# Gate and branch matmuls with tokens stationary and 512 weight columns moving

## The chip, the cores and the metric

The kernel runs on one core of one Trainium2 chip. The metric is device time in microseconds (us). TensorE does the matmuls; VectorE (DVE), ScalarE (ACT) and GpSimd (POOL) do the elementwise work; SyncE (SP) issues nearly all transfers. Each engine runs its own instructions in order, and engines wait for one another through semaphores.

## The reference, cut to what matters

Two layers of a hybrid encoder for 256 tokens of 1024 channels. The part of a layer that the change touches:

```python
h = rms_norm(x, g_mix)
... # out_a, out_b, out_c: three attentions of 4 heads; out_d: a convolution module; each (1, 256, 256)
branches = jnp.stack([out_a, out_b, out_c, out_d], axis=2)          # (1, 256, 4, 256)
proj = jnp.einsum('bsnc,ncd->bsnd', branches, w_branch)             # (1, 256, 4, 1024)
gates = jax.nn.sigmoid(h @ w_gate + b_gate).reshape(b, s, 4, 1024)  # w_gate: 1024 x 4096
x = x + jnp.sum(gates * proj, axis=2) @ w_o
hf = rms_norm(x, g_ffn)
x = x + jnp.square(jax.nn.relu(hf @ w_up)) @ w_down                 # 1024 -> 4096 -> 1024
```

All arrays are float32, and a final RMSNorm closes the trunk.

## The kernel before, in words

**Numbers and weights.** Each matrix product is made of three matmuls of float32r parts: a value is split into a high part (hi) and a remainder (lo), and high x high, high x low and low x high are added up in PSUM (`mm3`, lines 120 to 124). `weights` (line 102) brings one weight tile of 128x1024: SP starts the transfer into `raw` (5 buffers), ScalarE copies the high part (`hi`, line 114, 4 buffers), and VectorE subtracts (`lo`, line 115, 4 buffers). While `share[1]` is 2, POOL makes every second `lo`.

**Order of a layer.** The latent projection (`plat`, 4 tiles), the convolution's inputs (w_in tiles 10, 11, 8, 9), query and key tiles (`qk`), the values (4 tiles), the latent attention's up-projections (`mla`), four more `qk` tiles, 32 gate tiles, 8 branch tiles, 8 tiles of the output projection w_o, then the MLP. The order on TensorE is the order in which the code emits it. The other engines' orders are chosen by a list scheduler at build time, which simulates the program, so that an instruction emitted later can stand earlier in its engine's queue.

**Side work by ticks.** From `qk(0)` on, each weight tile ends with `tick()`, which emits the next entry of `side` (lines 675 to 698). The entries hold the twelve attention heads (`scores`, three ticks later `transposes`, one more tick later `weighted`, and the next head every two ticks, from tick A0 = 4 on), small preparations (the turned latents `plt` at ticks 1 to 3, the rotary key's rows `pkr` at 4, the rotary tables `pcs` at 5) and the convolution's taps at ticks 4 to 24, its normalization at 25 to 29. With A0 = 4 there are 31 entries: 13 tiles before the gates and 18 gate tiles carry them. When they are used up, `share[1]` becomes 0 and the branches start.

**Gates.** The normalized input is kept turned, `xg`, with channels in partitions and the 256 tokens as columns. A gate tile is a set of 128 output channels: its weights are stationary, 8 blocks of 128x128, and the 256 tokens move. `gates(g)` makes two such tiles in one PSUM buffer of the pool `pmm` (tag "mm", 4 buffers). VectorE multiplies by the row of token scales `rb` into `Z` (line 717). ScalarE adds the bias, one number per partition, in `sigmoids(m)` (line 722).

**Branches.** `branch(m)` makes 128 output channels of all four branches with one weight tile, again with weights stationary and 256 tokens moving. VectorE multiplies by the gates (line 737), POOL adds the four products (lines 738, 739), ScalarE and VectorE split the sum into `y` (lines 740, 741). With channels in partitions, `y` is already the form that the output projection takes.

**Output projection.** Lines 768 to 788: here blocks of 128 tokens of `y` are stationary and 512 columns of w_o move. Four PSUM buffers of "mm" hold the sums of the two token blocks and two column halves, over four pairs of k.

Other PSUM pools: `psc` ("sc", 1 buffer) and `ppv` ("pv", 1), which attention uses for scores and weighted values, and `pms` ("ms", 2), for turned tiles and small things.

Of the kernel before, what the change touches and what calls it, by code (L numbers as in the profile page):

```python
# [40 lines left out]
LAT = 420  # L41
WCOLS = 1024

C_GMIX, C_GFFN, C_BGATE, C_GQ, C_GKV, C_DW, C_BDW, C_GLN, C_BLN, C_BF = 0, 8, 16, 48, 50, 51, 113, 115, 117, 119
NSMALL = 123


A0 = 4
CONV_FROM, CONV_TO = 4, 25
WARM = 9  # L50

# [16 lines left out]


@with_exitstack  # L70
def hybrid_trunk(ctx: ExitStack, tc: tile.TileContext, xT, xtok, pos, small, gfin, abias, w_lat, w_v, w_in, w_uq, w_ukv,
                 w_gate, w_br, w_o, w_up, w_dn, out):
    nc = tc.nc

# [15 lines left out]
    def nm(s):  # L90
        count[0] += 1
        return f"{s}_{count[0]}"

    def after(inst, other):
        tc.add_manual_dep(inst.ins, other.ins.name,
                          mybir.DependencyInfo(mybir.DependencyClass.NoSync, mybir.DependencyReason.DATA),
                          reason="order")
# [4 lines left out]
    def weights(src, n=WCOLS, pieces=1, between=None):  # L102
        raw = rawp.tile([P, WCOLS], F32, tag="raw", name=nm("raw"))
        hi = whp.tile([P, WCOLS], F32R, tag="hi", name=nm("hi"))
        lo = wlp.tile([P, WCOLS], F32R, tag="lo", name=nm("lo"))
        share[0] += 1
        eng = nc.gpsimd if share[1] and share[0] % share[1] == 0 else nc.vector
        w = n // pieces
        for c in range(0, n, w):
            nc.sync.dma_start(raw[:, c:c + w], src[:, c:c + w])  # L110
            if c == 0 and between is not None:
                between()
        for c in range(0, n, w):
# [211 lines left out]
    for l in range(L):  # L325
        s = sm[l]

        def col(c):
            return s[:, c:c + 1]
# [191 lines left out]
        def conv_silu(prev):  # L521
            xc = cn["xc"]
            sg = tmp.tile([P, 2, T], F32, tag="d1", name=nm("dsg"), bufs=1)
            after(nc.scalar.activation(sg, xc, AF.Sigmoid), prev)
            nc.vector.tensor_tensor(xc, xc, sg, op=ALU.mult)
            nc.scalar.copy(br[0][:, 6:8, :], xc)
            nc.vector.tensor_tensor(br[1][:, 6:8, :], xc, br[0][:, 6:8, :], op=ALU.subtract)
# [177 lines left out]
        qk(4, True)  # L705
        qk(6, False)


        Z = [big.tile([P, 16, T], F32, tag="big", name=nm("Z")) for _ in range(2)]
        y = [None, None]  # L710

        def gates(g):
            ps = new_ps("pgt")
            for i in range(2):
                mtile(ps[:, i * T:(i + 1) * T], w_gate[l, 2 * g + i], xg)
            i = 2 * g % 16
            nc.vector.tensor_tensor(Z[g // 8][:, i:i + 2, :], ps2(ps), bc(rb, 2), op=ALU.mult)

        def sigmoids(m):
            for i in range(4 * m, 4 * m + 4):  # L720
                zt = Z[i // 16][:, i % 16, :]
                after(nc.scalar.activation(zt, zt, AF.Sigmoid, bias=col(C_BGATE + i)), last_exp[0])

        def branch(m):
            if m == 0:
                y[:] = [act.tile([P, 8, T], F32R, tag="qk1", name=nm("yh")),
                        act.tile([P, 8, T], F32R, tag="qk2", name=nm("yl"))]
            w = weights(w_br[l, m])
            yt = tmp.tile([P, 4, T], F32, tag="y4", name=nm("yt"))
            for a in range(2):  # L730
                ps = new_ps("pbr")
                for n in range(2):
                    for k in range(2):
                        i = 2 * (2 * a + n) + k
                        mm3(ps[:, n * T:(n + 1) * T], cols(w, i), part(br, i), k == 0, k == 1)
                i = (4 * m + 2 * a) % 16
                nc.vector.tensor_tensor(yt[:, 2 * a:2 * a + 2, :], ps2(ps), Z[m // 4][:, i:i + 2, :], op=ALU.mult)
            nc.gpsimd.tensor_tensor(yt[:, 0:2, :], yt[:, 0:2, :], yt[:, 2:4, :], op=ALU.add)
            nc.gpsimd.tensor_tensor(yt[:, 0, :], yt[:, 0, :], yt[:, 1, :], op=ALU.add)
            nc.scalar.copy(y[0][:, m, :], yt[:, 0, :])  # L740
            nc.vector.tensor_tensor(y[1][:, m, :], yt[:, 0, :], y[0][:, m, :], op=ALU.subtract)

        nbr = -1
        for g in range(16):
            gates(g)
            if side:
                continue
            share[1] = 0
            if nbr < 0:
                conv_silu(last_exp[0])  # L750
            else:
                branch(nbr)
            nbr += 1
            sigmoids(nbr)
        for m in range(nbr, KT):
            branch(m)
            if m + 1 < KT:
                sigmoids(m + 1)


        def tokens(ps, st, w, j, first, last):

            mm3(ps, st, (w[0][:, j * 512:(j + 1) * 512], w[1][:, j * 512:(j + 1) * 512]), first, last, late_mov=True)
# [1 line left out]
        def block(pair, k, b):  # L765
            return pair[0][:, k, b * P:(b + 1) * P], pair[1][:, k, b * P:(b + 1) * P]

        xg2 = new_xg()
        po = {(b, h): new_ps("po") for h in range(2) for b in range(NB)}

        def joined(b, h):

            xs = X[:, b, h * 512:(h + 1) * 512]
            nc.vector.tensor_tensor(xs, po[b, h], xs, op=ALU.add)

        def gffn(k):
            return col(C_GFFN + k)

        for kp, h in ((0, 0), (0, 1), (1, 0), (1, 1), (2, 0), (2, 1), (3, 0), (3, 1)):
            w = weights(w_o[l, kp, h])  # L780
            for b in range(NB):
                for j in range(2):
                    k = 2 * kp + j
                    tokens(po[b, h], block(y, k, b), w, j, k == 0, k == KT - 1)
                if kp == 3:
                    joined(b, h)
                    if (h, b) == (1, 0):
                        to_features(0, xg2, gffn, pms, "ms")
        v2 = stream_squares()
        rsq = tmp.tile([P, NB], F32, tag="rsq", name=nm("rsq"))  # L790
        nc.vector.reciprocal(rsq, v2)
# [176 lines left out]
```

## Time and profile before

| | us |
|---|---|
| median of 3 runs | 844.85 (843.68 to 844.89) |
| profiled execution | 845.43 |
| its span | 843.6 |
| TensorE busy in the span (matmuls) | 826.0 (98%) |
| VectorE | 569.9 (68%) |
| ScalarE | 450.0 (53%) |
| GpSimd | 152.7 (18%) |

The span is the profiled execution from its first to its last instruction; the rest of its own time lies around it. Matmuls overlap, so the duration of one in the trace is longer than the step from one start to the next; what they cost is read from the steps. PE is TensorE's matmuls and PEld its loads of the stationary operand.

### The profile page before, as it was taken

How to read it: one execution, taken by the hardware profiler on the slowest of the kernel's cores; microseconds unless marked ns; L12 is line 12 of the kernel's file. 1: busy time of each engine (PE TensorE's matmuls, PEld its weight loads, DVE VectorE, ACT ScalarE, POOL GpSimd, SP SyncE). 2: the span in 40 equal slices, each digit the busy share in tenths (PEclk: the TensorE clock that was granted, in tenths of full speed). 3: DMA queues.
4: the chain of work that ended last, by engine and by line, in shares of the span. 5: the costliest groups of instructions: out<-in, count | busy, mean ns of one | idle time of the engine just before them, and what ended most of it. 6: DMA issues, size and time to landing. Idle time of an engine off the chain costs nothing.

```text
span 843.6 us, 14520 instructions
## 1 busy us (share of the span) xinstructions
PE 826.0 (98%) x5646; PEld 759.5 (90%) x5646; DVE 569.9 (68%) x950; ACT 450.0 (53%) x759; POOL 152.7 (18%) x156
## 2 busy tenths in 40 slices
PE   9989999999999999999999999999999999999996
PEld 8969999999889999999899899999998899999994
DVE  7889984787665555555578899557866655555554
ACT  6745646654464444544485764485445554545443
POOL 6524332124200000000004332312331000000000
PEclk9999999999999999999999999999999999999999
DMA  8655433555546555555554544345555555555531
GB/s 281 232 181 181 132 126 126 166 184 185 165 164 198 189 189 186 186 189 187 172 176 161 188 132 145 132 131 174 194 176 200 175 186 190 191 185 186 188 126 50
DMA packets 42549, 145.55 MB, mean 173 GB/s; under 512 B 5104, under 2 KB 7408, under 8 KB 42352
## 3 DMA queue, kind: packets, MB, share of 16 engines
q1 hardware_dynamic: 41904, 142.98, 52.1%
q10 hardware_dynamic: 576, 1.64, 0.5%
q8 instruction: 44, 0.72, 0.4%
q14 instruction: 25, 0.20, 0.1%
HBM read 143.55 MB, written 1.05 MB: 171 GB/s over the span
## 4 chain that ended last, share of the span: by engine, by line
PE 89%; DVE 5%; issue 2%; POOL 1%; ACT 1%; DMA 0%; SPq 0%; POOLq 0%; DVEq 0%; ACTq 0%
PE pgt L122 7%; PE pgt L123 7%; PE pgt L124 7%; PE pu L123 7%; PE pu L124 7%; PE pu L122 7%; PE pd L123 7%; PE pd L122 7%; PE pd L124 7%; PE S L555 2%; DVE lo L115 2%; PE pqk L122 2%; PE pPV L593 2%; PE pqk L123 2%; PE pqk L124 2%
## 5 line engine op out<-in xcount | busy, mean ns | idle before, releaser
L115 DVE TENSOR_TENSOR lo<-raw,hi 128x1024 fp32r<-128x1024 f32 (+3 forms) x241 | 300.5, 1250 | 195.9 <-ACT hi L114 193.9
L114 ACT CAST hi<-raw 128x1024 fp32r<-128x1024 f32 (+2 forms) x273 | 278.5, 1024 | 266.0 <-issue 208.0
L122 PE MATMUL pgt<-xgh,hi 128*128 128x256 f32 x512 | 149.5, 292 | 0.0
L122 PE MATMUL pu<-xgh,hi 128*128 128x256 f32 x512 | 144.9, 283 | 0.7 <-ACT xgh L293 0.7
L123 PE MATMUL pu<-xgl,hi 128*128 128x256 f32 x512 | 145.1, 283 | 0.3
L124 PE MATMUL pu<-xgh,lo 128*128 128x256 f32 x512 | 144.9, 283 | 0.0
L123 PE MATMUL pgt<-xgl,hi 128*128 128x256 f32 x512 | 144.7, 283 | 0.0
L124 PE MATMUL pgt<-xgh,lo 128*128 128x256 f32 x512 | 144.7, 283 | 0.0
L122 PE MATMUL pd<-hi,u 128*128 128x512 f32 x256 | 100.8, 394 | 1.6 <-ACT u L803 1.6
L123 PE MATMUL pd<-hi,u 128*128 128x512 f32 x256 | 100.7, 393 | 1.1 <-DVE u L804 1.1
L122 PEld LDWEIGHTS pu<-xgh,hi 128*128 128x128 f32 x512 | 98.0, 191 | 3.4 <-ACT xgh L293 1.1
L123 PEld LDWEIGHTS pu<-xgl,hi 128*128 128x128 f32 x512 | 98.0, 191 | 3.0 <-DVE xgl L294 0.7
L124 PE MATMUL pd<-lo,u 128*128 128x512 f32 x256 | 99.6, 389 | 0.0
L122 PEld LDWEIGHTS pgt<-xgh,hi 128*128 128x128 f32 x512 | 97.9, 191 | 0.8 <-issue 0.3
L123 PEld LDWEIGHTS pgt<-xgl,hi 128*128 128x128 f32 x512 | 98.1, 192 | 0.4
L124 PEld LDWEIGHTS pu<-xgh,lo 128*128 128x128 f32 x512 | 98.0, 191 | 0.0
L124 PEld LDWEIGHTS pgt<-xgh,lo 128*128 128x128 f32 x512 | 97.9, 191 | 0.0
L115 POOL TENSOR_TENSOR lo<-raw,hi 128x1024 fp32r<-128x1024 f32 (+1 forms) x32 | 77.4, 2419 | 111.2 <-ACT hi L114 106.5
L491 DVE SCALAR_TENSOR_TENSOR cacc<-up,sm,cacc 128x256 f32<-128x256 f32 x120 | 77.9, 693 | 0.0
L122 PEld LDWEIGHTS pd<-hi,u 128*128 128x128 f32 x256 | 48.3, 189 | 10.8 <-ACT u L803 2.4
L124 PEld LDWEIGHTS pd<-lo,u 128*128 128x128 f32 x256 | 48.1, 188 | 10.4
L123 PEld LDWEIGHTS pd<-hi,u 128*128 128x128 f32 x256 | 48.3, 189 | 9.7 <-DVE u L804 2.0
(255 smaller groups left out, 1358.3 us busy)
## 6 DMA issues: line engine op xcount, KB each, us to landing
raw<-in_w_gate SPq DMA_DIRECT2D x64, 512.0 KB, 3.7
raw<-in_w_up SPq DMA_DIRECT2D x64, 512.0 KB, 4.2
raw<-in_w_dn SPq DMA_DIRECT2D x64, 512.0 KB, 4.2
raw<-in_w_in SPq DMA_DIRECT2D x23, 512.0 KB, 4.2
raw<-in_w_br SPq DMA_DIRECT2D x16, 512.0 KB, 3.7
raw<-in_w_o SPq DMA_DIRECT2D x16, 512.0 KB, 4.3
raw<-in_w_v SPq DMA_DIRECT2D x8, 512.0 KB, 4.2
raw<-in_w_lat SPq DMA_DIRECT2D x8, 210.0 KB, 4.6
```

The source lines that it names most:

```text
L114: cut = nc.scalar.copy(hi[:, c:c + w], raw[:, c:c + w])
L115: done = eng.tensor_tensor(lo[:, c:c + w], raw[:, c:c + w], hi[:, c:c + w], op=ALU.subtract)
L122: nc.tensor.matmul(ps, sh, mh, start=first, stop=False)
L123: nc.tensor.matmul(ps, *((sl, mh) if late_mov else (sh, ml)), start=False, stop=False)
L124: nc.tensor.matmul(ps, *((sh, ml) if late_mov else (sl, mh)), start=False, stop=last)
L491: ins = nc.vector.scalar_tensor_tensor(cacc[:, c, :], up[:, c, j:j + T], wcol, cacc[:, c, :], op0=ALU.mult, op1=ALU.add)
L555: nc.tensor.matmul(sl, q[:, b * P:(b + 1) * P], k[:, 0:n], start=True, stop=True)
L593: nc.tensor.matmul(po[o:o + 64, 0:T], v[:, 0, vo:vo + HD], pts[:, 0:T], start=True, stop=False)
```

## The change

The gates and the branches take the form of the output projection: token blocks of 128 are stationary, 512 weight columns move, and the results have tokens in partitions. `gates(c, i)` makes column half c of branch i's gate with four weight tiles into two PSUM buffers; VectorE scales each by the tokens' column `rc` and adds the bias, which now lies along the columns: a tile `bg` of 128x512, one buffer, brought by SP right after the set's first weight tile is asked for. `sigmoid` is one instruction for a set. `branch(c, i)` uses one weight tile, PSUM buffers of "sc" and "pv" (even i) or "ms" (odd i). The sum over the branches is made by POOL for i = 1 and 2 and by VectorE for i = 3. Since the output projection wants channels in partitions, `turned(c)` turns the sums by transposes on TensorE, 8 for each half, and ScalarE and VectorE split them into `y`. The turn of half 0 follows the last set of gates, that of half 1 follows four tiles of the output projection. A0 is 6 instead of 4: attention begins two weight tiles later, the entries of `side` become 33, and 20 gate tiles carry the last of them.

```diff
-A0 = 4
+A0 = 6
...
+        def tokens(ps, st, w, j, first, last):
+            mm3(ps, st, (w[0][:, j * 512:(j + 1) * 512], w[1][:, j * 512:(j + 1) * 512]), first, last, late_mov=True)
+        def block(pair, k, b):
+            return pair[0][:, k, b * P:(b + 1) * P], pair[1][:, k, b * P:(b + 1) * P]
...
-        def gates(g):
-            ps = new_ps("pgt")
-            for i in range(2):
-                mtile(ps[:, i * T:(i + 1) * T], w_gate[l, 2 * g + i], xg)
-            i = 2 * g % 16
-            nc.vector.tensor_tensor(Z[g // 8][:, i:i + 2, :], ps2(ps), bc(rb, 2), op=ALU.mult)
...
+        Z = [big.tile([P, 4, NB, 512], F32, tag="big", name=nm("Z")) for _ in range(2)]
+        def gates(c, i):
+            ps = [new_ps("pgt") for _ in range(NB)]
+            bg = tmp.tile([P, 512], F32, tag="bg", name=nm("bg"), bufs=1)
+            for kp in range(4):
+                w = weights(w_gate[l, c, i, kp])
+                if kp == 0:
+                    nc.sync.dma_start(bg, bgate[l, c, i])
+                for b in range(NB):
+                    for j in range(2):
+                        k = 2 * kp + j
+                        tokens(ps[b], block(xg, k, b), w, j, k == 0, k == KT - 1)
+                tick()
+            for b in range(NB):
+                nc.vector.scalar_tensor_tensor(Z[c][:, i, b, :], ps[b], rc[:, b:b + 1], bg, op0=ALU.mult, op1=ALU.add)
+        def sigmoid(c, i):
+            after(nc.scalar.activation(Z[c][:, i], Z[c][:, i], AF.Sigmoid), last_exp[0])
+        def branch(c, i):
+            pools = (((psc, "sc"), (ppv, "pv")), ((pms, "ms"), (pms, "ms")))[i % 2]
+            ps = [pool.tile([P, 512], F32, tag=tag, name=nm("pbr")) for pool, tag in pools]
+            w = weights(w_br[l, c, i])
+            for b in range(NB):
+                for j in range(2):
+                    tokens(ps[b], block(br, 2 * i + j, b), w, j, j == 0, j == 1)
+                nc.vector.tensor_tensor(Z[c][:, i, b, :], ps[b], Z[c][:, i, b, :], op=ALU.mult)
+                if i == 3:
+                    nc.vector.tensor_tensor(Z[c][:, 0, b, :], Z[c][:, 0, b, :], Z[c][:, 3, b, :], op=ALU.add)
+            if i in (1, 2):
+                nc.gpsimd.tensor_tensor(Z[c][:, 0], Z[c][:, 0], Z[c][:, i], op=ALU.add)
+        def turned(c):
...
+            for pr in range(2):
+                pt = pms.tile([P, 512], F32, tag="ms", name=nm("pyt"))
+                for j in range(2):
+                    o = (2 * pr + j) * P
+                    for b in range(NB):
+                        nc.tensor.transpose(pt[:, j * T + b * P:j * T + (b + 1) * P], Z[c][:, 0, b, o:o + P], ident)
+                ks = slice(4 * c + 2 * pr, 4 * c + 2 * pr + 2)
+                nc.scalar.copy(y[0][:, ks, :], ps2(pt))
+                nc.vector.tensor_tensor(y[1][:, ks, :], ps2(pt), y[0][:, ks, :], op=ALU.subtract)
...
+        raw_gates, todo = [], [(0, i) for i in range(4)]
+        for c, i in [(c, i) for c in range(2) for i in range(4)]:
+            gates(c, i)
+            raw_gates.append((c, i))
+            if side:
+                continue
+            first = share[1] != 0
+            if first:
+                share[1] = 0
                 conv_silu(last_exp[0])
+            while raw_gates:
+                sigmoid(*raw_gates.pop(0))
+            if first:
+                continue
+            for _ in range(2):
+                if todo:
+                    branch(*todo.pop(0))
+        turned(0)
...
+        branch(1, 0)
+        branch(1, 1)
+        output(0, 0)
+        branch(1, 2)
+        branch(1, 3)
+        output(0, 1)
+        output(1, 0)
+        output(1, 1)
+        turned(1)
+        for kp, h in ((2, 0), (2, 1), (3, 0), (3, 1)):
+            output(kp, h)
```

`output(kp, h)` is the body of the former loop over w_o's tiles; its PSUM buffers are now taken one by one, at kp = 0. On the host w_gate, w_branch and the bias are laid out for the new tiles, and the bias leaves the table of small constants.

## Rows read from the trace of the kernel before

**Rows 1.** The profile page, chain that ended last: shares by engine.
```profile
PE 89%; DVE 5%; issue 2%; POOL 1%; ACT 1%; DMA 0%; SPq 0%; POOLq 0%; DVEq 0%; ACTq 0%
```

**Rows 2.** Busy time by stretch: start:end, length, busy us by engine, clock, DMA.
```profile
46.00:50.00 4.00, 0.71 (x4) 0.28 (x2) 4.00 (x6) 1.04 (x1) 1.31 (x1) 1.00 0.26 85
154.00:191.00 37.00, 37.00 (x309) 36.75 (x308) 28.58 (x32) 20.11 (x29) 9.53 (x7) 1.00 0.54 174
```

**Rows 3.** Groups of instructions by shape: count | busy us, mean ns | idle before.
```profile
L122 PE MATMUL pgt<-xgh,hi 128*128 128x256 f32 x512 | 149.5, 292 | 0.0
...
L122 PE MATMUL pbr<-brh,hi 128*128 128x256 f32 x128 | 36.2, 283 | 0.0
```

**Rows 4.** Timeline of TensorE in gates: start us, us, instruction.
```profile
189.78 0.28 PE L122 MATMUL pgt<-xgh,hi 128*128 128x256 f32 x1
...
194.70 0.28 PE L124 MATMUL pgt<-xgh,lo 128*128 128x256 f32 x1
```

**Rows 5.** Timeline of TensorE in the output projection and at transposes of X.
```profile
221.63 0.40 PE L124 MATMUL po<-lo,yh 128*128 128x512 f32 x1
...
223.25 0.39 PE L122 MATMUL po<-hi,yh 128*128 128x512 f32 x1
...
238.66 0.39 PE L124 MATMUL po<-lo,yh 128*128 128x512 f32 x1
238.90 1.03 PE L303 MATMUL pt<-ident,X 128*128 128x128 f32 x8
239.69 0.48 PE L122 MATMUL po<-hi,yh 128*128 128x512 f32 x1
240.00 0.39 PE L123 MATMUL po<-hi,yl 128*128 128x512 f32 x1
```

**Rows 6.** Timeline of ScalarE after those transposes.
```profile
239.53 0.91 ACT L293 ACTIVATE xgh<-pt,sm 128x256 fp32r<-128x256 f32 x2 [0.97 <-PE pt L303]
```

**Rows 7.** ScalarE's copies of 512 columns, line 526: ns min/median/max.
```profile
L526 ACT CAST brh<-xc x2: 607/607/607, 156.2 to 566.8; 128x512 fp32r<-128x512 f32 x2
```

**Rows 8.** Instructions of tile yt: ns min/median/max, first and last start.
```profile
L737 DVE TENSOR_TENSOR yt<-pbr,Z x32: 677/682/691, 162.6 to 631.5; 128x512 f32<-128x512 f32 x32
L738 POOL TENSOR_TENSOR yt<-yt x16: 1292/1296/2378, 164.1 to 632.3; 128x512 f32<-128x512 f32 x16
```

**Rows 9.** Timeline of VectorE after the transposes of X.
```profile
240.34 0.87 DVE L294 SCALAR_TENSOR_TENSOR xgl<-pt,sm,xgh 128x256 fp32r<-128x256 f32 x2
```

**Rows 10.** Timeline of TensorE where the output projection starts.
```profile
220.38 0.39 PE L124 MATMUL po<-lo,yh 128*128 128x512 f32 x1
221.09 0.47 PE L122 MATMUL po<-hi,yh 128*128 128x512 f32 x1 [0.31 <-DVE yt L737]
```

**Rows 11.** Timeline of SP's queue in layer 0 (stretch, instructions merged).
```profile
43.84 5.72 SPq L110 DMA_DIRECT2D raw<-in_w_in  x3
53.13 0.33 SPq L558 DMA_DIRECT2D bt<-in_abias  x1
```

**Rows 12.** Timeline of SP's queue, the output weights of layer 0.
```profile
197.55 20.27 SPq L110 DMA_DIRECT2D raw<-in_w_o  x8
```

**Rows 13.** Timeline of TensorE at the first scores of layer 0.
```profile
46.23 0.39 PE L124 MATMUL pv<-lo,xgh 128*128 128x512 f32 x1
49.91 0.92 PE L555 MATMUL S<-qkA 64*128 64x128 f32 x4 [3.29 <-DVE qkA L636]
...
51.26 0.63 PE L123 MATMUL pv<-hi,xgl 128*128 128x512 f32 x1
...
54.67 0.40 PE L122 MATMUL pv<-hi,xgh 128*128 128x512 f32 x1
```

**Rows 14.** Timeline of VectorE before these scores.
```profile
38.20 3.35 DVE L115 TENSOR_TENSOR lo<-raw,hi 128x1024 fp32r<-128x1024 f32 x1
...
48.65 0.47 DVE L294 SCALAR_TENSOR_TENSOR latl<-plt,sm,lath 128x256 fp32r<-128x256 f32 x1
```

**Rows 15.** The profile page, transfers: count, KB each, us to landing.
```profile
raw<-in_w_gate SPq DMA_DIRECT2D x64, 512.0 KB, 3.7
```

More of the change, by code (lines that the diff above doesn't have):

```diff
@@ L42 @@
 WCOLS = 1024
-C_GMIX, C_GFFN, C_BGATE, C_GQ, C_GKV, C_DW, C_BDW, C_GLN, C_BLN, C_BF = 0, 8, 16, 48, 50, 51, 113, 115, 117, 119
-NSMALL = 123
-A0 = 4
+C_GMIX, C_GFFN, C_GQ, C_GKV, C_DW, C_BDW, C_GLN, C_BLN, C_BF = 0, 8, 16, 18, 19, 81, 83, 85, 87
+NSMALL = 91
+A0 = 6
 CONV_FROM, CONV_TO = 4, 25
@@ L70, in hybrid_trunk @@
 @with_exitstack
-def hybrid_trunk(ctx: ExitStack, tc: tile.TileContext, xT, xtok, pos, small, gfin, abias, w_lat, w_v, w_in, w_uq, w_ukv,
+def hybrid_trunk(ctx: ExitStack, tc: tile.TileContext, xT, xtok, pos, small, gfin, bgate, abias, w_lat, w_v, w_in, w_uq, w_ukv,
                  w_gate, w_br, w_o, w_up, w_dn, out):
@@ L706, in hybrid_trunk @@
         qk(6, False)
-        Z = [big.tile([P, 16, T], F32, tag="big", name=nm("Z")) for _ in range(2)]
-        y = [None, None]
-        def gates(g):
-            ps = new_ps("pgt")
-            for i in range(2):
-                mtile(ps[:, i * T:(i + 1) * T], w_gate[l, 2 * g + i], xg)
-            i = 2 * g % 16
-            nc.vector.tensor_tensor(Z[g // 8][:, i:i + 2, :], ps2(ps), bc(rb, 2), op=ALU.mult)
[L719 to L758, printed above, removed]
         def tokens(ps, st, w, j, first, last):
@@ L766, in block @@
             return pair[0][:, k, b * P:(b + 1) * P], pair[1][:, k, b * P:(b + 1) * P]
+        Z = [big.tile([P, 4, NB, 512], F32, tag="big", name=nm("Z")) for _ in range(2)]
+        y = []
+        def gates(c, i):
[12 more added lines that the diff above has]
+                nc.vector.scalar_tensor_tensor(Z[c][:, i, b, :], ps[b], rc[:, b:b + 1], bg, op0=ALU.mult, op1=ALU.add)
@@ new lines, in turned @@
+        def turned(c):
+            if c == 0:
+                y[:] = [act.tile([P, 8, T], F32R, tag="qk1", name=nm("yh")),
+                        act.tile([P, 8, T], F32R, tag="qk2", name=nm("yl"))]
+            for pr in range(2):
[7 more added lines that the diff above has]
+                nc.vector.tensor_tensor(y[1][:, ks, :], ps2(pt), y[0][:, ks, :], op=ALU.subtract)
@@ new lines, in hybrid_trunk @@
+        raw_gates, todo = [], [(0, i) for i in range(4)]
[7 more added lines that the diff above has]
+                share[1] = 0
+                conv_silu(last_exp[0])
+            while raw_gates:
[5 more added lines that the diff above has]
+                    branch(*todo.pop(0))
@@ L768, in hybrid_trunk @@
+        assert not todo
+        turned(0)
         xg2 = new_xg()
-        po = {(b, h): new_ps("po") for h in range(2) for b in range(NB)}
+        po = {}
         def joined(b, h):
@@ L774, in joined, with output @@
             nc.vector.tensor_tensor(xs, po[b, h], xs, op=ALU.add)
-        def gffn(k):
-            return col(C_GFFN + k)
-        for kp, h in ((0, 0), (0, 1), (1, 0), (1, 1), (2, 0), (2, 1), (3, 0), (3, 1)):
+        def output(kp, h):
             w = weights(w_o[l, kp, h])
             for b in range(NB):
+                if kp == 0:
+                    po[b, h] = new_ps("po")
                 for j in range(2):
@@ L788, in hybrid_trunk, with gffn @@
                         to_features(0, xg2, gffn, pms, "ms")
+        def gffn(k):
+            return col(C_GFFN + k)
+        branch(1, 0)
[9 more added lines that the diff above has]
+            output(kp, h)
         v2 = stream_squares()
@@ L940 @@
     ukv = np.concatenate([ukv[..., :HD].reshape(L, P, 256), ukv[..., HD:].reshape(L, P, 256)], axis=2)
-    gate = A(w_gate).reshape(L, KT, P, 4, KT, P).transpose(0, 4, 3, 2, 1, 5).reshape(L, 32, P, D)
-    bgate = A(b_gate).reshape(L, 4, KT, P).transpose(0, 3, 2, 1).reshape(L, P, 32)
-    brw = A(w_branch).reshape(L, 4, 2, P, KT, P).transpose(0, 4, 3, 1, 2, 5).reshape(L, KT, P, D)
+    gate = A(w_gate).reshape(L, 4, 2, P, 4, 2, 512).transpose(0, 5, 4, 1, 3, 2, 6).reshape(L, 2, 4, 4, P, D)
+    bgate = A(b_gate).reshape(L, 4, 2, 512).transpose(0, 2, 1, 3)[:, :, :, None, :]
+    bgate = np.broadcast_to(bgate, (L, 2, 4, P, 512))
+    brw = A(w_branch).reshape(L, 4, 2, P, 2, 512).transpose(0, 4, 1, 3, 2, 5).reshape(L, 2, 4, P, D)
     dn = A(w_down).reshape(L, FT, P, D)
@@ L948 @@
     bf = np.broadcast_to(A(b_forget)[:, None, :], (L, P, HEADS))
-    small = np.concatenate([pk(g_mix), pk(g_ffn), bgate, pk(g_q_lat), pk(g_kv_lat), dw, pk(b_dw), pk(g_conv_ln),
+    small = np.concatenate([pk(g_mix), pk(g_ffn), pk(g_q_lat), pk(g_kv_lat), dw, pk(b_dw), pk(g_conv_ln),
                             pk(b_conv_ln), bf], axis=2)
@@ L956 @@
         xT=A(x).reshape(T, KT, P).transpose(2, 1, 0), xtok=A(x).reshape(NB, P, D).transpose(1, 0, 2), pos=A(positions).reshape(NB, P).T, small=small,
-        gfin=np.broadcast_to(A(g_final)[None], (P, D)), abias=abias, w_lat=wlat, w_v=wv, w_in=win_t, w_uq=uq, w_ukv=ukv, w_gate=gate,
+        gfin=np.broadcast_to(A(g_final)[None], (P, D)), bgate=bgate, abias=abias, w_lat=wlat, w_v=wv, w_in=win_t, w_uq=uq, w_ukv=ukv, w_gate=gate,
         w_br=brw, w_o=wo, w_up=wt(w_up), w_dn=dn)
```

## The prediction

> **What bounds the kernel now.** I read the chain of waits first: 89% of what ended last is TensorE, so the time is TensorE's instructions plus the few places where it waits [rows 1]. Then the stretches: from 154 to 191 us, gates and branches alone, TensorE is busy all 37 us and VectorE 28.58 of them, so VectorE has a quarter to spare; from 46 to 50 us TensorE works only 0.71 us while VectorE works all 4 [rows 2]. So in the changed stages the pace of single matmuls counts, and in one place of layer 0 VectorE's backlog.
>
> **Gates and branches, 512 columns instead of 256.** Before: 512 gate matmuls in each of three groups, 1536, and 3 x 128 = 384 branch matmuls, all of 256 columns [rows 3]. After: a set has 4 x 2 x 2 x 3 = 48 matmuls of 512, with 8 sets and 2 layers 768; a branch 2 x 2 x 3 = 12, in all 192. The columns streamed stay the same, 960 instructions go.
> The price of one is from its start to the next start, since matmuls overlap. Gates: 189.78 to 194.70 in 41 steps, 0.120 us [rows 4]. The output projection already has tokens stationary and 512 columns moving, the form that the gates take: 223.25 to 238.66 in 68 steps, 0.2266; just before, 221.63 to 223.25 in 7 steps, 0.2314 [rows 5]. At 2.4 GHz 256 and 512 columns are 106.7 and 213.3 ns, so both forms carry some 13 ns beyond their columns, and one of two such remainders goes. Per pair 0.240 - 0.2266 = 13.4 ns, or 8.6 ns at the slower stretch; I take 12 ns, since only a few steps are at the slower pace. 960 x 12 ns = 11.5 us gained (8.3 to 12.9).
> The Trainium skill speaks against this size: "TensorE: Matmul & The Clock Gate", section "Back-to-back issue gap", gives 262 cycles for 256 columns and 518 for 512, so 6 cycles or 2.5 ns a pair; as an estimate from that page the gain would be 2.4 us and the sum about 846 us. The trace does not agree: 120 ns and 227 ns stand where the page's cycles make 109 and 216.
>
> **The sums turned by TensorE.** New: per layer 2 x 8 transposes of 128x128. The same 8 transposes of X between output matmuls run from 238.90 to 239.69, and the step after them is 0.31 instead of 0.227: 0.88 us for 8 [rows 5]. Four such groups: 3.5 us added, and nothing of it beside other work of TensorE.
> After turned(0) TensorE goes on with branch(1,0), which does not need y; output(0,0), which does, comes two weight tiles (5.4 us) later. Branch(1,1) wants the two "ms" buffers of turned(0) 2.7 us (12 matmuls) later; two copies and two subtractions fit in. I cost that at nothing; without the cover it is about the wait of turned(1).
> After turned(1) output(2,0) needs its result at once. In the like place the transposes start at 238.90 and ScalarE's copy at 239.53 [rows 5, 6], 0.63 later; a 512-wide copy takes 0.607 [rows 7], a 512-wide operation of VectorE 0.68 [rows 8]. High part ready 1.24 us after the start, low part some 2.0; TensorE is free after 0.85 and asks for the low part one matmul after the high one: 0.4 + 0.6 = 1.0 us of wait with both engines free. In the like place VectorE began 1.44 us after the transposes [rows 9]; a weight copy and a weight subtraction in front (twice a 512-wide one, 1.2 us each) would add 2.2. I take 1.7, nearer to the free case, twice: 3.4 us added (2.0 to 6.4).
>
> **Waits for the sums.** Turned(1) needs branch(1,3)'s products, POOL's two 1024-wide adds and VectorE's last two adds. From the end of branch(1,1) to turned(1) TensorE has six weight tiles, 6 x 12 x 0.2266 = 16.3 us. POOL's 512-wide add takes 1.3, at worst 2.38 us [rows 8]; two of double width 5.2 to 9.5. With 2.2 us ahead of them (a product behind a weight subtraction) and 3.8 behind (two adds of 0.68, each behind one), 11 to 15.5 us. It fits: nothing. Turned(0) has a whole set, 11 us, more.
> VectorE's other work: as many evictions and products as before, a layer's 8 splits of 256 become 4 of 512, and 4 adds are new (2.7 us); the spare quarter hides them [rows 2]. ScalarE's 32 sigmoids of 256 a layer become 8 of 1024, less work. Without that cover 2.7 us a layer would show. The smaller table of constants changes only a transfer at the start.
>
> **The wait that goes at the end.** Before, the output projection takes all four "mm" buffers while branch(7) still holds one: 220.38 to 221.09 is 0.71 instead of 0.23, 0.48 us [rows 10]. Branches now use other buffers. Two layers: 0.95 us gained (0 to 0.95).
>
> **The bias rows on SP's queue.** 16 new transfers of 256 KB go into a single buffer. Each waits until the set before has been evicted, and the weights behind it on SP wait too, and for them the two halves and TensorE. SP's order is not the program's: the third bias of attention stands in the program ahead of the four w_in tiles of qk(4) and qk(6), yet three w_in were issued from 43.84 on and it at 53.13 [rows 11]. And SP is far ahead: the first output weight was issued at 197.55 [rows 12], while its twelfth matmul starts at 220.38 [rows 10]. So a wait of a few us on SP is covered, and the bias itself has a set (11 us) to land. I take nothing; without cover, see the last rival.
>
> **Attention two tiles later.** In layer 0 TensorE waits from 46.46 to 49.91 for the first scores, 3.45 us, behind VectorE's qkA; then 8 matmuls take 0.427 us each, 512 columns at 1.2 GHz, 1.6 us more: 5.05 in all [rows 13]. With scores two tiles later this wait goes. What is late next: pkr's transposes, which now come first after that tile. They need a "ms" buffer, which plt's second tile holds until its latl ends, 48.65 + 0.47 = 49.12 [rows 14]. If VectorE's order there (a lo that took 3.35 us, then taps of the convolution) stays, TensorE still waits 2.65 us and only 0.8 us is gained, with the lower clock perhaps avoided. I take 2.0, nearer to that end (0.7 to 5.05). The tiles that carry attention grow from 31 to 33: work is moved, none added, and conv_silu and the branches begin after set 5, with their own time on TensorE unchanged.
>
> **The sum**, against the profiled run's own 845.43 us (span 843.6): -11.5 + 3.5 + 3.4 - 0.95 - 2.0 = -7.55, so 837.9; the median of the three runs is 844.85, 0.58 lower, so 837.3. I say 837. All ends for it: 844.85 - 12.9 + 3.5 + 2.0 - 0.95 - 5.05 = 831.5; all against: 844.85 - 8.3 + 3.5 + 6.4 - 0.7 = 845.8.
>
> **Rivals.**
> A, the wide matmuls don't pay: in the gates, beside more work of the other engines, they run at 0.2314 or slower, as the seven steps of the output do [rows 5]. At 0.2314 throughout 8.3 us remain and the time is 840.5, the edge of my own range; at 0.240, as long as two narrow ones, nothing remains: 848.8. Half way: 844.5. For it: the slower stretch exists. Against it: 68 steps at 0.2266.
> B, layer 0's wait goes wholly, with the clock: 3.05 us more, 834; with quick turns (2.0 instead of 3.4) 832.5. For it: a clear late comer, qkA, is taken off the path. Against it: the "ms" buffer at 49.12.
> C, slower: turned(1) waits for the sums. Every us by which the 11 to 15.5 us exceed the 16.3 us of cover is a us of TensorE, in each layer; it turns the sign from 4 us on. With 5 us and the lower clock behind it (1.6 us, rows 13) twice: 13 us, 850. For it: with adds of POOL at 2.38 us less than 1 us of cover is left. Against it: most take 1.3.
> D, slower: the bias transfer stands on SP ahead of its set's second to fourth tiles, so these are issued only after the set before is evicted: 1 us for that, 3.7 for the transfer [rows 15], 1.2 and 1.2 for the halves, less 2.7 for the tile in hand: 4.4 us a set, 16 sets, 70 us: 907. For it: it is so in the program. Against it: the order in rows 11.
>
> **How the numbers follow.** The likeliest 0.52 (own range 834.5 to 840.5), A 0.12, B 0.22, C 0.09, D 0.05. Some 0.2% (1.7 us) is what a measurement of this kernel can tell from no change. Faster: 0.52 + 0.22 + half of A = 0.80; the rest of A is 0.05 within and 0.01 slower; C and D are 0.14 slower. The range 831 to 846 leaves out C and D and the far end of A.
>
> **What would show it.** Gate steps of 0.227, 768 of them, and branch steps alike. Eight transposes in 0.8 us twice a layer; no wait after the first group, 1 to 3 us before the output matmul after the second. Layer 0's wait at 46.5 shorter, ended by latl and not by qkA, and 1.2 GHz after it or not. No wait of TensorE on a weight's halves in the gates. The prediction is wrong if steps of 512 columns in the gates lie above 0.232, if TensorE waits over 3 us at a turn, or if a bias transfer on SP stands before a gap of TensorE.

## The result, and the profile after

The changed kernel takes 849.63 us (median; 848.85 to 850.43) against 844.87 beside it: ratio 1.0059 [1.0041, 1.0076]. It is slower, where I forecast 837 (831 to 846). Its profiled execution has 849.28 us, span 847.5, of which TensorE is busy for 820.7 (97%): 5 us less work, and 9 us more in which it has none.

TensorE's waits in the changed kernel (us in total, times, longest):

```profile
PE pqk L124 <- POOL lo L115: 4.8, 1, 4.8
PE pPV L593 <- ACT pts L584: 3.2, 3, 1.2
PE po L123 <- DVE yl L763: 1.7, 2, 0.9
...
PE po L122 <- ACT yh L762: 1.0, 2, 0.5
```

The wait for qkA [rows 13] and the one where the output projection starts [rows 10] are gone. The two on `po` are turned(1), expected. The two longest were in no step of mine: a weight's low part from GpSimd, and the weighted values of attention.

The matmuls themselves did what was expected. Groups by shape (count | busy us, mean ns | idle before), where [rows 3] had 512 and 128 per line with 256 columns:

```profile
L122 PE MATMUL pgt<-hi,xgh 128*128 128x512 f32 x256 | 106.1, 415 | 0.0
...
L122 PE MATMUL pbr<-hi,brh 128*128 128x512 f32 x64 | 25.1, 392 | 0.0
...
L748 POOL TENSOR_TENSOR Z<-Z 128x1024 f32<-128x1024 f32 x8 | 20.8, 2600 | 123.6 <-DVE Z L744 101.1 <-ACT hi L114 22.5
```

TensorE's timeline in the gates, first beside attention, then after it, and at the two turns (start us, us, instruction, [idle before <- releaser]):

```profile
109.20 0.39 PE L123 MATMUL pgt<-hi,xgl 128*128 128x512 f32 x1
...
111.50 0.39 PE L124 MATMUL pgt<-lo,xgh 128*128 128x512 f32 x1
...
178.90 0.39 PE L122 MATMUL pgt<-hi,xgh 128*128 128x512 f32 x1
...
189.55 0.39 PE L124 MATMUL pgt<-lo,xgh 128*128 128x512 f32 x1
...
206.10 1.03 PE L760 MATMUL pyt<-ident,Z 128*128 128x128 f32 x8
206.89 0.48 PE L122 MATMUL pbr<-hi,brh 128*128 128x512 f32 x1
...
228.76 1.03 PE L760 MATMUL pyt<-ident,Z 128*128 128x128 f32 x8
230.31 0.51 PE L122 MATMUL po<-hi,yh 128*128 128x512 f32 x1 [0.52 <-ACT yh L762]
231.68 0.50 PE L123 MATMUL po<-hi,yl 128*128 128x512 f32 x1 [0.87 <-DVE yl L763]
```

47 steps from 178.90 to 189.55 make 0.2266 us each, and beside attention 10 steps from 109.20 to 111.50 make 0.230 (the 512-column pace of [rows 5], against 0.120 for 256 [rows 4]). After the first turn nothing waits: 0.79 us for 8 transposes, as in [rows 5]. After the second, 0.68 us lie between the transposes' 0.87 and the high part's matmul, and the step behind it is 1.37 instead of 0.227: 1.82 us a layer.

The loss starts in layer 0, in the second tile of qk(2). TensorE's timeline, and two windows of the same place (columns as in [rows 2], TensorE's, its weight loads', then the other engines' busy time, clock, DMA):

```profile
41.22 0.28 PE L123 MATMUL pqk<-xgl,hi 128*128 128x256 f32 x1
46.34 0.58 PE L124 MATMUL pqk<-xgh,lo 128*128 128x256 f32 x1 [4.85 <-POOL lo L115]
...
48.64 0.41 PE L122 MATMUL pqk<-xgh,hi 128*128 128x256 f32 x1
48.86 0.41 PE L123 MATMUL pqk<-xgl,hi 128*128 128x256 f32 x1
```

```profile
46.00:50.00 4.00, 3.66 (x19) 3.66 (x20) 0.00 (x0) 0.00 (x0) 2.62 (x2) 0.57 0.67 201
41.00:46.00 5.00, 0.49 (x5) 0.29 (x3) 3.09 (x6) 1.42 (x2) 2.38 (x3) 1.00 0.33 126
```

A step of 5.12 us stands where 0.12 is usual, and for some 3 us afterwards the granted clock is at the 1.2 GHz level: 0.21 us a step. Together about 6.5 us; the 5.05 us of [rows 13] are gone. The reason is in GpSimd's queue, and behind it in SyncE's. First the changed kernel, GpSimd and SyncE:

```profile
38.57 0.23 POOL L560 MEMSET bt<- 64x64 f32 x2 [5.51 <-DMA bt<-in_abias]
43.62 0.23 POOL L560 MEMSET bt<- 64x64 f32 x2 [4.82 <-DMA bt<-in_abias]
43.81 4.80 POOL L115 TENSOR_TENSOR lo<-raw,hi 128x1024 fp32r<-128x1024 f32 x2
```

```profile
29.26 3.87 SPq L110 DMA_DIRECT2D raw<-in_w_v  x3
33.18 0.44 SPq L558 DMA_DIRECT2D bt<-in_abias  x1
35.96 0.33 SPq L110 DMA_DIRECT2D raw<-in_w_v  x1
36.34 0.43 SPq L558 DMA_DIRECT2D bt<-in_abias  x1
```

Then the same two queues of the kernel before:

```profile
33.10 0.23 POOL L560 MEMSET bt<- 64x64 f32 x2 [0.50 <-DMA bt<-in_abias]
37.86 0.23 POOL L560 MEMSET bt<- 64x64 f32 x2 [4.53 <-DMA bt<-in_abias]
38.06 5.75 POOL L115 TENSOR_TENSOR lo<-raw,hi 128x1024 fp32r<-128x1024 f32 x2
```

```profile
29.18 0.42 SPq L558 DMA_DIRECT2D bt<-in_abias  x1
30.06 2.61 SPq L110 DMA_DIRECT2D raw<-in_w_v  x2
32.72 0.43 SPq L558 DMA_DIRECT2D bt<-in_abias  x1
```

In both kernels the planner put the masking of the first two heads' bias (`bt`) ahead of the low part that qk(2) wants. Before, both biases were issued by 32.72 and the low parts began at 38.06, in time. With attention two tiles later the first bias stands behind two more weight tiles on SyncE and the second behind one more; they are issued at 33.18 and 36.34, the second takes 7.2 us to land instead of 5.1, and the low parts begin at 43.81.

The other loss is at the weighted values, in both layers. TensorE, VectorE and ScalarE of the changed kernel in layer 1:

```profile
493.39 0.28 PE L124 MATMUL pqk<-xgh,lo 128*128 128x256 f32 x1
494.88 0.65 PE L593 MATMUL pPV<-pts,VAC 128*64 128x256 f32 x2 [1.22 <-ACT pts L584]
...
498.34 0.63 PE L123 MATMUL pgt<-hi,xgl 128*128 128x512 f32 x1
498.77 0.63 PE L124 MATMUL pgt<-lo,xgh 128*128 128x512 f32 x1
```

```profile
487.11 3.41 DVE L491 SCALAR_TENSOR_TENSOR cacc<-up,sm,cacc 128x256 f32<-128x256 f32 x3
490.44 1.72 DVE L634 SCALAR_TENSOR_TENSOR QC<-pqk,rb 64x256 f32<-64x256 f32 x4
492.20 0.29 DVE L570 CUSTOM_DVE_ANT_0 neg<-S,bt 128x128 f32<-128x128 f32 x1
```

```profile
492.53 0.40 ACT L572 ACTIVATE pe<-neg,mn 128x128 f32<-128x128 f32 x1 [5.74 <-DVE mn L570]
...
494.36 0.47 ACT L584 COPY pts<-pT 128x384 f32<-128x384 f32 x1
```

VectorE does three taps of the convolution and four evictions of QC before the next head's scores. ScalarE stands 5.74 us before that head's exp, and the copy `pts` of the head before, which TensorE wants at 493.5, is queued behind it. Price: 1.38 us here and at 82.6 us, 1.0 at 114.6, and in layer 1 a stretch at the 1.2 GHz level (0.43 us a step), 1.7 us more. In the kernel before, VectorE reached the scores emitted with the same weight tile after 2.1 us of such work instead of 5.1:

```profile
485.51 1.26 DVE L491 SCALAR_TENSOR_TENSOR cacc<-up,sm,cacc 128x256 f32<-128x256 f32 x3
486.69 0.85 DVE L634 SCALAR_TENSOR_TENSOR QC<-pqk,rb 64x256 f32<-64x256 f32 x2
487.58 0.29 DVE L570 CUSTOM_DVE_ANT_0 neg<-S,bt 128x128 f32<-128x128 f32 x1
```

Of the 3.0 us more, 0.9 are two more evictions of QC. The other 2.1 are the first of the three taps alone: in the changed kernel it starts just behind the start of a low part on GpSimd, which runs until 489.45, and ends only after it, at 489.73; the two taps behind it take 0.48 us each. In the kernel before, the low part starts when the taps are over, at 486.76, and the evictions beside it keep their 0.43 us. First GpSimd and VectorE of the changed kernel, then GpSimd of the kernel before:

```profile
487.06 2.39 POOL L115 TENSOR_TENSOR lo<-raw,hi 128x1024 fp32r<-128x1024 f32 x1
487.11 2.62 DVE L491 SCALAR_TENSOR_TENSOR cacc<-up,sm,cacc 128x256 f32<-128x256 f32 x1
```

```profile
486.76 2.40 POOL L115 TENSOR_TENSOR lo<-raw,hi 128x1024 fp32r<-128x1024 f32 x1 [3.90 <-ACT hi L114]
```

### The profile page after: what moved, and what is told of

The parts are those of the page before. It is cut to its first block, busy times and chain, and to the rows that moved or that the text cites. A ratio compares the mean times of both kernels' runs of the same rounds, so it can differ in the third digit from the quotient of the medians.

```text
span 847.5 us, 12604 instructions
## 1 busy us (share of the span) xinstructions
PE 820.7 (97%) x4718; PEld 710.5 (84%) x4718; DVE 579.4 (68%) x948; ACT 438.2 (52%) x703; POOL 132.2 (16%) x134
## 5 line engine op out<-in xcount | busy, mean ns | idle before, releaser
L122 PE MATMUL pgt<-hi,xgh 128*128 128x512 f32 x256 | 106.1, 415 | 0.0
L123 PE MATMUL pgt<-hi,xgl 128*128 128x512 f32 x256 | 100.5, 393 | 0.0
L124 PE MATMUL pgt<-lo,xgh 128*128 128x512 f32 x256 | 100.5, 393 | 0.0
L115 POOL TENSOR_TENSOR lo<-raw,hi 128x1024 fp32r<-128x1024 f32 (+1 forms) x34 | 81.0, 2384 | 109.5 <-ACT hi L114 104.8
L491 DVE SCALAR_TENSOR_TENSOR cacc<-up,sm,cacc 128x256 f32<-128x256 f32 x120 | 83.2, 735 | 0.0
L124 PEld LDWEIGHTS pgt<-lo,xgh 128*128 128x128 f32 x256 | 48.5, 189 | 11.0
L122 PEld LDWEIGHTS pgt<-hi,xgh 128*128 128x128 f32 x256 | 48.5, 189 | 10.5 <-issue 1.3
L123 PEld LDWEIGHTS pgt<-hi,xgl 128*128 128x128 f32 x256 | 48.6, 190 | 9.2
```

What stands on the lines that cost most here:

```text
L491: ins = nc.vector.scalar_tensor_tensor(cacc[:, c, :], up[:, c, j:j + T], wcol, cacc[:, c, :], op0=ALU.mult, op1=ALU.add)
```

## The experiments

Each ratio is to the kernel before on the same chip, with its 95% interval; "us" is the median.

**Attention back at 4.** The change with one number undone.

```diff
-A0 = 6
+A0 = 4
```

> The changed kernel with A0 = 4 again. Theory 1 (attention two tiles later made the loss): the waits of the changed kernel at 41 us (5.0 us on POOL's lo and 1.6 us of lower clock), at the weighted values (1.3, 1.0, 1.3 us) and the lower clock of layer 1 (1.7 us) go, and the 5.05 us wait for the first scores comes back: 849.6 less 6.5, 842 to 844. Theory 2 (the bias rows' 4 MB and their waits on SP delay the other transfers, or the wide gates don't pay; A0 matters little): 848 to 850, with waits of TensorE on weights.

Measured: 840.31 us, ratio 0.9944 [0.9926, 0.9963]. The waits for GpSimd's low part and at the weighted values are gone; qkA's is back at 1.85 us, with the lower clock behind it, and is TensorE's longest wait:

```profile
PE S L555 <- DVE qkA L636: 1.9, 1, 1.9
```

So the new tiling gains, and A0 alone costs 1.0059 - 0.9944 = 1.15%, 9.7 us.

**A0 = 6 in the kernel before.** The other half of the same split.

```diff
-A0 = 4
+A0 = 6
```

> The kernel before with A0 = 6 alone, nothing else of the change. Theory 1: the same new waits without the new gates: in layer 0 a wait of about 5 us on POOL's lo in place of the one for the first scores, waits of about 1 us at the weighted values, a lower clock in one or two places: 846 to 851. Theory 2: no new wait, 844 to 845, or 840 if the old wait goes and nothing follows.

Measured: 857.75 us, 1.0146 [1.0127, 1.0165]: 12.3 us, more than any theory had. The wait on GpSimd's low part is there at 5.6 us, with eight waits at the weighted values, 6.4 us together, and the clock stays at the 1.2 GHz level for longer (from 46 to 52 us at least, a granted clock of 0.50). A0's cost does not need the new tiles.

**The bias early.** The first two heads' bias loaded and masked before w_in's tile 11.

```diff
+        for h in range(2):
+            bts[h] = load_bias(h)
...
-                bt = tmp.tile([P, 3 * P], F32, tag="bt", name=nm("bt"))
-                nc.sync.dma_start(bt, abias[l, h])
...
+                bt = bts.pop(h) if h in bts else load_bias(h)
```

> The changed kernel (A0 = 6) with the attention biases of heads 0 and 1 loaded and masked before w_in tile 11, so that POOL does not stand behind their transfers. Theory 1: the wait at 41 us and its lower clock go (6.6 us), two transfers of 192 KB more at the start cost up to 1.4: 843 to 845; the waits at the weighted values stay. Theory 2: POOL's lo comes late because the weights land late: the wait stays, 848 to 851.

Measured: 846.43 us, 1.0011 [0.9997, 1.0025]. The wait on the low part went, and in its place TensorE waits for the "ms" buffers, by its timeline:

```profile
45.29 0.44 PE L426 MATMUL plt<-ident,qn 128*128 128x128 f32 x2 [1.17 <-DVE latl L294]
50.80 0.44 PE L449 MATMUL pkr<-ident,kr 128*128 128x128 f32 x2 [2.32 <-DVE latl L294]
```

The second is the wait that the prediction named (latl before pkr): it was right about what is late next in VectorE's chain and blind to GpSimd's, which came first.

**The second turn one tile earlier.**

```diff
-        output(1, 1)
         turned(1)
+        output(1, 1)
```

> The changed kernel with the second turn before the last of the four output tiles instead of after it. The sums were complete at 224.0 us, the turn would start at 226.0 instead of 228.7. Theory 1 on the turn (copy and subtraction are the wait): both waits of 1.86 us go, 845.5 to 846.5. Rival (the sums are late, VectorE behind POOL): the wait moves to the front of the transposes, 849 to 850.

Measured: 845.46 us, 1.0005 [0.9993, 1.0016]: 0.54% or 4.6 us less than the change, both waits on `po` gone. They are 3.7 us in the trace, within the intervals.

**The taps two ticks later as well.**

```diff
-CONV_FROM, CONV_TO = 4, 25
+CONV_FROM, CONV_TO = 6, 27
```

> The changed kernel (849.3 us beside a kernel before of 845.4) with attention still at tick 6, and the convolution's taps moved two ticks later as well (ticks 6 to 26 instead of 4 to 24), so that taps and heads keep the distance that they had before the change. Theory 1 (of the about 9 us that A0 = 6 costs, the lo on GpSimd that stands behind the bias of the heads is 5.0 us with 1.6 us of lower clock, and the waits at the weighted values, 1.4 and 1.0 us in each layer, come from VectorE's order, in which taps and all four evictions of QC stand ahead of a head's scores): the wait of 5 us at 41.2 us stays, and the waits at 82.6, 114.6 and 493.4 us shrink only in so far as the taps make them, because the evictions of QC still stand ahead: 846 to 849 us. Rival (it is the distance between taps and heads that was lost): all waits at the weighted values go with the lower clock after them in layer 1: about 843 us.

Measured: 851.38 us, 1.0074 [1.0057, 1.0090]. No better than the change, perhaps a little worse. The waits at the weighted values are six instead of three, 5.7 us in all. VectorE's order ahead of the head's scores is the same three taps, the first of them behind a low part of GpSimd, and four evictions. Moving the ticks of the taps did not change the order that the planner made; whether that order is what costs is tried further down.

**Attention at 4 with the earlier turn, and then with the taps from 6 on.** Two kernels; the second has both edits and this one.

```diff
-CONV_FROM, CONV_TO = 4, 25
+CONV_FROM, CONV_TO = 6, 25
```

> The changed kernel with attention at tick 4 as before the change (840.3 us) and the second half of the sums turned one tile of the output projection earlier, so that the last such tile stands between the transposes and the matmul that needs their result. Theory 1 (the two measures touch different places and add up; the turn's wait and its slow first step are 1.86 us a layer): 836.6 us. Rival (the sums are now wanted 2.7 us sooner and TensorE waits for GpSimd's adds instead): 840 us or more.

> The kernel with attention at tick 4 and the second turn one tile earlier (theory: 836.6 us), and the convolution's taps from tick 6 on instead of 4 (62 taps over 19 ticks), so that fewer taps stand ahead of qkA's eviction on VectorE in layer 0. Theory 1 (the 2.0 us at the first scores with the 1.6 us of lower clock behind it are VectorE's backlog of taps): both go, 833 us. Rival (the wait moves to the next tile that wants an "ms" buffer, as in the run with the bias early): 835 to 838 us.

Measured: 838.23 us, 0.9918 [0.9902, 0.9934], and 834.77 us, 0.9880 [0.9861, 0.9898]. The two measures add up, though 2.2 us are left of the 3.7; in the trace of the first kernel a wait of 0.68 us for one of GpSimd's low parts is new. In the second kernel the wait for qkA is shorter, not gone (1.38 us instead of 1.87).

**Without the bias rows**, at A0 = 4; the gates' bias is left out.

```diff
+    bg = cst.tile([P, 512], F32, name="bg")
+    nc.gpsimd.memset(bg, 0.0)
...
-            bg = tmp.tile([P, 512], F32, tag="bg", name=nm("bg"), bufs=1)
...
-                    nc.sync.dma_start(bg, bgate[l, c, i])
```

> The changed kernel with attention at tick 4 (840.3 us), without the 16 transfers of the gates' bias rows: the bias is left out of the gates (a constant tile of zeros is added in its place). It prices the transfers on SyncE's queue, which I put at nothing. Theory 1: 840.3 us within 1 us. Rival (the transfers delay weights somewhere): 837 to 838.5 us.

Measured: 842.50 us, 0.9975 [0.9963, 0.9986], slower than with the bias. The trace has a new wait of 2.0 us at the start, on GpSimd's sums, which the tile of zeros now stands ahead of; without it the run would be where the other was, 840.5. The experiment brought its own cost, so it does not price the transfers by itself. With the trace of the changed kernel, in which no matmul of the gates waits for a weight, I take them as hidden.

**Low parts ahead of the bias masks on GpSimd**, A0 = 6. One order edge; SyncE's order stays the changed kernel's.

```diff
-                    nc.gpsimd.memset(bt[...], NEG)
+                    after(nc.gpsimd.memset(bt[...], NEG), pool_lo[0])
```

> The changed kernel (A0 = 6, 849.3 us beside a kernel before of 844.9) with one order edge on GpSimd alone: the memsets that mask a head's bias stand behind every lo that the program emitted before them, as the program has it. SyncE's order stays that of the changed kernel. Theory 1 (the 5.0 us at 41.2 us come from GpSimd's queue, in which those memsets wait for the bias while the lo of a weight stands behind them): this wait goes (with its 1.6 us of lower clock), and the next late comer, the "ms" buffers that plt and pkr need, shows as in the run with the bias early, 1.3 and 2.5 us: 846 to 848 us. If nothing is late behind it: 843 us. Rival (the lo is late for another reason, its raw tile lands too late): no change, 849 us. The waits at the weighted values stay in each case.

Measured: 843.55 us, 0.9980 [0.9971, 0.9989]: 6.7 us less than the change (1.0059 - 0.9980 = 0.79%). GpSimd's queue, where the low parts now begin 6.4 us sooner and the mask follows them (the numbers of lines are 1 to 3 higher in this kernel):

```profile
37.44 5.83 POOL L116 TENSOR_TENSOR lo<-raw,hi 128x1024 fp32r<-128x1024 f32 x2 [4.35 <-ACT hi L115]
43.20 0.23 POOL L563 MEMSET bt<- 64x64 f32 x2
```

TensorE's wait in qk(2) is gone, with SyncE issuing the two biases when it did before (33.21 and 36.38). This shows the first cause: GpSimd's order, not late weights. The edge names nothing else, but the planner shifted VectorE's order a little with it: the waits at the weighted values are four instead of three, 3.1 us against 3.2. The "ms" waits hardly came (0.21 us); another did, 1.67 us for qkB at 62.8 us.

**Scores ahead of QC and KC on VectorE**, A0 = 6.

```diff
+                    if last_neg[0] is not None:
+                        after(ins, last_neg[0])
```

(after each eviction of qk; `last_neg` is the last head's scores emitted.)

> The changed kernel (849.3 us) with order edges on VectorE: the evictions of QC and KC stand behind the scores of the last head emitted before them. Taps are left as they are. Theory 1 (the four evictions of QC ahead of head 2's scores, 1.72 us, are what makes TensorE wait 1.38 us at 82.6 and 493.4 us): both waits go, with the lower clock after the second (1.7 us); the wait at 114.6 us and the 5.0 us at 41.2 us stay: 844.5 to 846.5 us. Rival (the taps, slowed to 1.1 us each by GpSimd's lo, are enough by themselves): the waits stay at about 1 us, 848 to 849 us.

Measured: 849.04 us, 1.0055 [1.0038, 1.0071]. The rival was right. VectorE's order shows why:

```profile
486.95 4.59 DVE L492 SCALAR_TENSOR_TENSOR cacc<-up,sm,cacc 128x256 f32<-128x256 f32 x6
491.46 0.28 DVE L572 CUSTOM_DVE_ANT_0 neg<-S,bt 128x128 f32<-128x128 f32 x1
```

Three more taps took the place of the evictions; the scores come 0.74 us sooner, and the two waits only halve (1.22 to 0.62 and 0.66 us of idle time), while one of 0.82 us is new at 526 us. The rival's reason was not quite right: the six taps take 4.59 us because the first stands behind GpSimd's low part (2.61), and the others take 0.47 each.

**Scores ahead of the taps too**, the same edge in `conv`.

> As the run before (QC and KC behind the scores), with the convolution's taps also behind the scores of the last head emitted before them. Theory 1 (what stands ahead of a head's scores on VectorE is the whole of the waits at the weighted values): all of these go, 1.0 us a layer more than in the run before, and the 5.0 us at 41.2 us stay: 842.5 to 844.5 us. Rival (the taps that are pushed back come back as a wait elsewhere, at the convolution's sums or at the lo of a weight): 846 us or more.

Measured: 844.73 us, 0.9995 [0.9985, 1.0005]: 5.4 us less than the change. All waits at the weighted values are gone, and nothing came back elsewhere; the wait in qk(2) stays (4.8 us).

**All edges together**, A0 = 6.

> The changed kernel with A0 = 6 and all order edges: lo ahead of the bias masks on GpSimd, scores ahead of QC, KC and taps on VectorE. Theory 1 (these two queue orders are the whole cost of A0 = 6): 849.3 - 6.6 - 4.7 - 1.7 = 836.3 us, plus what the "ms" buffers still cost in layer 0 (0 to 3.8 us): 836 to 840 us, no more than the 840.3 us of the kernel with attention at tick 4. Rival (later attention costs by itself, through work pushed into the gates): 843 us or more.

Measured: 837.31 us, 0.9909 [0.9896, 0.9922]. No wait in attention is left. The two queue orders are the whole cost of A0 = 6: 0.79% and 0.64% alone, 1.50% together. That is more than the 1.15% that A0 cost; the next run shows that the same edges also gain at A0 = 4.

**All edges with A0 = 4**, to price later attention by itself.

> The kernel with all order edges (837.3 us with A0 = 6, beside a kernel before of 845.2), with A0 = 4. It prices later attention by itself, with neither queue order against it: the term that I forecast at -2.0 us (0.7 to 5.05). Theory 1 (with the orders held, later attention does gain what stands at the first scores of layer 0: 1.9 us of wait in the run with attention at tick 4, and 1.6 us of lower clock with it): 839 to 841 us. Rival (the edges alone take the taps from in front of qkA, and the wait goes at A0 = 4 as well): 837 us or less, and A0 = 6 is worth nothing.

Measured: 837.45 us, 0.9905 [0.9889, 0.9922], the same as with A0 = 6. The rival was right: with the taps behind the scores VectorE evicts qkA in time at A0 = 4 as well, so later attention is worth nothing.

**The same edges in the kernel before.**

> The kernel before (A0 = 4, narrow gates) with the same order edges. It tells how much of the 7.9 us between the kernel before and the run with all edges is the edges' own. Theory 1 (the kernel before loses nothing by its orders but a part of the 3.4 us and the lower clock at the first scores of layer 0): 842 to 845 us. Rival (the taps behind the scores free VectorE ahead of qkA wholly): 840 us, the whole 5.05 us.

Measured: 840.77 us, 0.9946 [0.9930, 0.9961]: 4.6 us, about the 5.05 of [rows 13]. The wait that A0 = 6 was to remove went by an order of VectorE and GpSimd, at no price. Between this kernel and the one above only the tiling differs: 0.9905 / 0.9946 = 0.9959, 3.5 us (the medians differ by 3.3).

**All edges and the earlier turn.**

> The kernel with all order edges and A0 = 6 (837.3 us), and the second half of the sums turned one tile of the output projection earlier. Theory 1 (the two turn waits, 0.71 + 1.15 us a layer, go as in the two runs that had this edit before, by 2.2 and 4.2 us in their medians): 833 to 835 us. Rival (the sums are late now that attention ends two tiles later): 837 us or more.

Measured: 833.31 us, 0.9859 [0.9840, 0.9878], the lowest of all, though its interval overlaps that of the run at 834.77; it beats both the kernel before and the change.

## Why the prediction was wrong, step by step

What TensorE spends, as the sum of the steps from each matmul's start to the next, by the tile of the first (us, after less before; worked out from all matmuls of the traces):

| tile | the change | same edges, A0 = 4 in both |
|---|---|---|
| pgt (gates) | -5.0 | -8.3 |
| pbr (branches) | -2.4 | -2.4 |
| pyt (turned sums) | +4.7 | +4.7 |
| po (output projection) | +1.3 | +1.4 |
| pqk | +9.1 | 0.0 |
| pv | -5.1 | 0.0 |
| all matmuls | +2.8 | -3.5 |

The right column is the tiling without the queues' disturbance. In the left one waits of attention fall on pqk and pgt. The profiled spans differ by 3.8, the last 1.0 us of it behind the last matmul. That is not chance: the stretch behind the last matmul's start is 7.45 us in all three runs with the old tiles, 7.8 with the new ones at A0 = 4 and 8.3 to 8.5 with the new ones at A0 = 6. Its cause stays open.

- **Wide matmuls, -11.5 (8.3 to 12.9): nearly right.** Gates -8.3 and branches -2.4 make -10.7. The branches have my 12 ns a pair (2.4 / 192 = 12.3); the gates 10.8, since those beside attention run at 0.230, near the slower pace of [rows 5]. From the cycles that the Trainium skill's page "TensorE: Matmul & The Clock Gate", section "Back-to-back issue gap", gives for isolated matmuls, one gets as an estimate 2.5 ns a pair, 2.4 us in all; this trace does not agree, since both forms still carry their 13 ns.
- **Transposes, +3.5: right.** 32 of 109 ns.
- **Turned(1), +3.4: right in size**, with 1.82 us a layer, and nothing at turned(0). That it fell between my two ends is partly luck: a weight copy and a weight subtraction did stand in front, the case that I had priced at 3.2 us a layer (with 2.2 for two operations of 1.2, which is 2.4). But the copy ran mostly during the transposes, and only the subtraction (1.23 us) showed.
- **Sums' wait, 0: right.** GpSimd's adds of 1024 take 2.60 us (a 512-wide one at 1.29 doubled), and the turn does not wait for them. (The 2.2 us for a product behind a weight subtraction is 1.9 by its own terms, 0.68 and 1.2; nothing hangs on it.) Rival C did not occur.
- **Wait at the output projection, -0.95: right;** it is gone, inside the +1.3 of po.
- **Bias rows, 0: right** as far as the runs show: no matmul of the gates waits for a weight, and leaving the rows out gained nothing. Rival D did not occur.
- **Attention two tiles later, -2.0 (0.7 to 5.05): this is the step that failed.** It is +9.7 us in the changed kernel, and outside of its own range on the other side. I followed the wait for qkA to what is late next, and only in VectorE's chain: the latl that it found became a wait only when GpSimd's was taken away. What moved with A0 were also the bias transfers of the heads (SyncE), their masks (GpSimd, with weights' low parts behind them in the same queue), and each head's scores against taps and evictions on VectorE, with ScalarE's copies behind the exp. I wrote "work is moved, none added", as if moved work were free. The rows that would have warned were in the trace before: GpSimd's low parts began at 38.06, right behind a mask that had waited 4.53 us for its bias.
- **No rival had it.** B took the same term to the good side; those on the slow side (A, C, D) were about the new tiles, and so were the three signs of being wrong; the third, a bias transfer on SyncE before a gap of TensorE, came true only by biases of attention, which it did not mean. Without the A0 term my sum was -5.55; the tiling measures -3.3 to -3.5, and the difference is mostly in the wide matmuls (0.8) and in 0.9 us of longer steps at a wait for the convolution's scales (`pb`), which the runs with the new tiles and A0 = 4 have and those with A0 = 6 don't.

The 837 us that I forecast is what the change takes once the two queues keep their order (837.31), but that is chance in part: the way there is the edges' -4.6 and the tiling's -3.5, not mine.

## What to carry to other kernels

A step that is moved takes its transfers and its small instructions on every engine along; for each queue ask what stands behind them that did not wait before, above all behind an instruction that waits for a transfer. Where a planner orders the queues, one number that shifts emission re-sorts all of them: hold the orders with explicit edges, try each part of a change alone, and judge the tiling between kernels with the same edges. A wait that seems to need a shift of the work may need only an order.

## What the runs showed of the hardware that I had not expected

VectorE is not slowed evenly where GpSimd works beside it: one instruction stands still, and those behind it pay nothing. Of the 19 taps of the changed kernel that start while GpSimd makes a low part, 18 end 0.28 us after that low part, however early they began, and take 1.40 to 2.62 us; the nineteenth began in the same instant and took 0.47, as taps do with no low part beside them (0.46 to 0.48). The mean of a merged row (3.41 us for three taps, 1.1 each) hides this. Not every instruction is held: in the kernel before, beside the low part at 486.76, the evictions of QC take 0.43 us and the scores 0.29, as elsewhere. The strongest case is in the run with the bias early, where GpSimd made two low parts, until 40.44 and until 42.80: two operations of VectorE on 8 columns ended at 40.47 and 42.84. Below them stands the first of the two as it runs in the kernel before, with no low part beside it:

```profile
38.07 2.40 DVE L462 TENSOR_TENSOR e<-z,e 128x8 f32<-128x8 f32 x1
40.51 2.33 DVE L466 TENSOR_SCALAR lfc<-e 128x8 f32<-128x8 f32 x1
```

```profile
35.96 0.15 DVE L462 TENSOR_TENSOR e<-z,e 128x8 f32<-128x8 f32 x1
```

And the lower clock does not follow from the length of a wait alone. With attention at 4 a wait of 1.85 us at the first scores was followed by a granted clock of 0.54 (50 to 52 us); with the earlier turn added, an edit far behind this place, the same wait of 1.87 us was followed by 1.00 throughout. Nor need the edit be the reason: executions of one kernel differ as much. The six of the kernel with the earlier turn took 836.20 to 839.27 us, at mean granted clocks of 0.998 to 0.994. A trace shows one execution, so the 1.6 or 1.7 us of lower clock read from it are in some executions of a kernel and not in others.
